# Ten norm factors take a way through scratch memory in place of a TensorE spread

## The chip, the cores and the metric

The kernel runs on one core of a Trainium2 chip. The time is device microseconds of one execution. The core's engines are TensorE (PE in the profile, its weight loads PEld), VectorE (DVE), ScalarE (ACT), GpSimd (POOL) and SyncE (SP); SP and ACT issue the DMAs, which sixteen DMA engines carry out. Each engine works through its own list of instructions in the order of the program; an instruction that has to wait holds up those behind it on its engine.

## The reference

One layer of an encoder over 2048 tokens of 1024 features: a gated short convolution, then a SwiGLU network of 2816 hidden features, each between two RMS norms and scaled, shifted and gated by vectors made from `c`.

```python
def rms_norm(x, g):
    y = x * lax.rsqrt(jnp.mean(x * x, axis=-1, keepdims=True) + RMS_EPS)
    return y * g

h = modulate(rms_norm(x, gains[0]), sh_m, sc_m)
h = short_conv_mixer(h, w_in, w_conv, w_out)       # 1024 -> 3072, conv of width 3, 1024 -> 1024
x = x + g_m * rms_norm(h, gains[1])
h = modulate(rms_norm(x, gains[2]), sh_f, sc_f)
h = swiglu(h, w_gate_up, w_down)                   # 1024 -> 5632, 2816 -> 1024
x = x + g_f * rms_norm(h, gains[3])
```

A norm's factor `rsqrt(mean + eps)` is one number per token, and it multiplies every feature of that token.

## The kernel before

Features lie on the 128 partitions and 512 tokens along the free axis. The 2048 tokens are two halves (`u` = 0, 1) of two token tiles each (`tok` = 0, 1) of 512. The eight phases in program order are in0, out0, in1, out1, gu0, down0, gu1, down1: the convolution's input and output projection for both halves, then the gate-up and down projection for both halves. Each product of 2x2 blocks is done by Strassen's seven products (P1 to P7), and each fp32 product as three matmuls on operands split into a high and a low part (`h` and `l` in tile names).

The work is a list of slots, one per product, about twelve matmuls of 128x512 each. The main loop walks the slots; in front of a slot it issues the supply of coming weights, the events scheduled for that slot, and whatever `later(n, f)` has put off by `n` slots; a generator that does `yield n` is resumed `n` slots later. Every engine keeps this order: nothing is reordered by a scheduler.

A factor is made by `norm_of_sums`: four tiny matmuls sum the squares over the partitions, so that token 128 t + p of the tile has its sum on partition p in column t, and a few tiny DVE and POOL instructions make `q`, 128x4, out of it. To multiply a 128x512 tile whose tokens lie along the free axis, the factors must stand as one row of 512 that is the same in all 128 partitions. That is what `spread_later` makes: `diagonal` writes four 128x128 blocks, the identity times a column of `q` (four DVE instructions); four slots later `spread` multiplies a 128x128 matrix of ones with the 128x512 result on PE into a PSUM bank, and ACT copies the bank into an SBUF tile `rb`, of which there are two buffers (`NRB`).

Fourteen factors are spread. Names: `r0` to `r3` for the first norm of each token tile; `n00` to `n11` (after out0 and out1, digits `u` and `tok`) for the second; `m00` to `m11` are the factors of the third, spread under the names `h00` to `h11` before gu0 and gu1; `o00` and `o01` (after down0) and `o10` (during down1) for the fourth; the very last one is made and spread by `last_half`. A tile name ends in `q` for the 128x4 factor, `d` for the diagonal, `b` for the PSUM bank and `r` for the row in all partitions.

Users of a row: after n, `after_out` loads the stored output tiles (`zz`) and input tiles (`xx`), multiplies `zz` by the row on DVE, adds, and stores the sum as `x1`. After h, `Features.scale` multiplies the tiles of the gu phase (`gu0a` to `gu0d`, `gu1a` to `gu1d`). After o, `after_down` finishes the output tiles (`zo`, `xo`).

DMAs of the stretch that the prediction speaks of: `in6P3k` and the like are kept weight operands of in1 loaded by SP, `kgu2P` the gu weights split ahead during in1 and stored by SP (ACT writes their buffers next), `y1A` and `y1S` stored operands for out1, `ada` rows for the conditioning vectors.

Of the kernel before, what the change touches and what calls it, by code (L numbers as in the profile page):

```python
# [10 lines left out]
F32 = mybir.dt.float32  # L11
# [4 lines left out]
P = 128  # L16
# [7 lines left out]
CH = 512  # L24
# [11 lines left out]
NBIG, NWP, NRAW, NTMP, NRB = 17, 7, 16, 10, 2  # L36
# [13 lines left out]
def hybrid_conv_layer(  # L50
# [31 lines left out]
    V, A, PE, G, SP = map(Engine, (nc.vector, nc.scalar, nc.tensor, nc.gpsimd, nc.sync))  # L82
# [4 lines left out]
    bigs, pairs, raws, sb = (ctx.enter_context(tc.tile_pool(name=n, bufs=1)) for n in ("bigs", "pairs", "raws", "sb"))  # L87
# [6 lines left out]
    def raw(name):  # L94
        return raws.tile([P, CH], F32, tag="raw", bufs=NRAW, name=name)
# [7 lines left out]
    def small(n, name):  # L103
        return sb.tile([P, n], F32, tag="small", bufs=16, name=name)

    def bank(name):
        return ps.tile([P, CH], F32, tag="mm", bufs=8, name=name)
# [5 lines left out]
    def later(slots, f):  # L113
        waiting.append((now[0] + slots, len(waiting), f))

    def run(gen):


        def step():
            n = next(gen, None)  # L120
            if n is not None:
                later(n, step)

        step()
# [38 lines left out]
    def col(t, k):  # L163
        return t[:, k : k + 1]
# [53 lines left out]
    def root(v, name):  # L218

        p, t = small(4, name + "p"), small(4, name + "t")  # L220
        G.tensor_tensor(p, v, mhalf, ALU.pow)
        yield 1
        q = sb.tile([P, 4], F32, tag="q", bufs=8, name=name + "q")
        V.tensor_tensor(t, p, p, ALU.mult)
        V.tensor_tensor(t, t, v, ALU.mult)
        V.scalar_tensor_tensor(q, t, -3.0, p, ALU.add, ALU.mult)
        return q
# [8 lines left out]
    def diagonal(q, name):  # L236
        dg = tmp(name + "d")
        for t in range(4):
            V.tensor_scalar(dg[:, t * P : (t + 1) * P], ident, q[:, t : t + 1], None, ALU.mult)
        return dg  # L240

    def spread(dg, name):
        ps_ = bank(name + "b")
        PE.matmul(ps_, one, dg[:, :CH], start=True, stop=True)
        rb = sb.tile([P, CH], F32, tag="rb", bufs=NRB, name=name + "r")
        A.copy(rb, ps_)
        return rb

    def spread_later(q, name, put, lag=4):
        dg = diagonal(q, name)  # L250
        yield lag
        put(spread(dg, name))

    def norm_of_sums(acc, name):

        st = bank(name + "s")
        for t in range(4):
            PE.matmul(st[:, t : t + 1], acc[:, t * P : (t + 1) * P], mean, start=True, stop=True)
        v = small(4, name + "v")
        V.tensor_scalar(v, st[:, :4], EPS, None, ALU.add)  # L260
        yield 1
        return (yield from root(v, name))
# [29 lines left out]
    def scratch(shape, name):  # L292
        return dram.tile(shape, F32, name=name)
# [586 lines left out]
    def schedule(slot, f):  # L880
        events.setdefault(max(slot, 0), []).append(f)
# [10 lines left out]
    for s in slots:  # L892
        ph = s.ph
        if ph.kind in ("out", "down"):
            w = Weight(ph.kind, s.grp, s.op, None, ks=s.ks)
        elif s.n < LEAD and ph.name != "in0" or ph.name == "in1" and s.g.i == 2:
            w = Weight(ph.kind, s.grp, s.op, None)
        else:
            b = of.setdefault((ph.name, s.n), Blocks(ph.kind, s.grp))
            w = Weight(ph.kind, s.grp, s.op, b, ph.name == "in0" and s.g.i in (1, 2),  # L900
                       whole_words=ph.name == "in0" and s.n < LEAD and s.op in UNSPLIT)
# [3 lines left out]
        if s.n >= LEAD and extra.get(ph.name) and len(position) > 7 * LEAD + 2 * (EARLY - LEAD):  # L905
            n = count[ph.name] = count.get(ph.name, 0) + 1
# [24 lines left out]
    rb1 = {}  # L931

    def put(d, key, rb):
        d[key] = rb

    def after_out(ph, tok):

        u = ph.u
        rb = {}
        yield 7  # L940
        q = yield from norm_of_sums(ph.acc[tok], f"n{u}{tok}")
        yield (24 if u == 0 else 34) + 8 * tok
        yield from spread_later(q, f"n{u}{tok}", partial(put, rb, 0))
        acc = {}
        tiles = {}

        def load(k):
            z, xt = raw(f"zz{u}{tok}{k}"), raw(f"xx{u}{tok}{k}")
            SP.dma_start(z, z_d[u][tok][:, k, :])
            SP.dma_start(xt, xt_d[u * 2 + tok, k // 4][:, (k % 4) * CH : (k % 4 + 1) * CH])  # L950
            tiles[k] = z, xt

        load(0)
        yield 1
        load(1)
        yield 2
        for k in range(KD):
            if k + 2 < KD:
                load(k + 2)
            z, xt = tiles.pop(k)  # L960
            V.scalar_tensor_tensor(z, z, col(mG[0], k), rb[0], ALU.mult, ALU.mult)
            V.tensor_tensor(xt, xt, z, ALU.add)
            later(2, partial(add_square, acc, 0, xt, f"nq{u}{tok}{k}"))
            later(3, partial(A.dma_start, x1_d[u][tok][:, k, :], xt))
            yield 2
        yield 7
        rb1[u, tok] = yield from norm_of_sums(acc[0], f"m{u}{tok}")

    def after_down(ph, tok):
        u = ph.u  # L970
        rb = {}
        if ph.last and tok:
            yield 1
            yield from last_half(ph)
            return
        yield 4 if ph.last else 7
        q = yield from norm_of_sums(ph.acc[tok], f"o{u}{tok}")
        if not ph.last:
            yield 22 + 10 * tok
        yield from spread_later(q, f"o{u}{tok}", partial(put, rb, 0), 2 if ph.last else 4)  # L980
        tiles = {}

        def load(k):
            xt = raw(f"xo{u}{tok}{k}")
            SP.dma_start(xt, x1_d[u][tok][:, k, :])
            if ph.last:
                z = ph.z(tok, k)
            else:
                z = raw(f"zo{u}{tok}{k}")
                SP.dma_start(z, z2_d[u][tok][:, k, :])  # L990
            tiles[k] = z, xt

        load(0)
        yield 1
        load(1)
        yield 2
        for k in range(KD):
            if k + 2 < KD:
                load(k + 2)
            z, xt = tiles.pop(k)  # L1000
            V.scalar_tensor_tensor(z, z, col(mG[1], k), rb[0], ALU.mult, ALU.mult)
            V.tensor_tensor(xt, xt, z, ALU.add)
            later(1, partial(A.dma_start, out_tile(u, tok, k), xt))
            yield 1.5 if ph.last else 2

    def out_tile(u, tok, k):
        return out[u * 2 + tok, k // 4][:, (k % 4) * CH : (k % 4 + 1) * CH]
# [44 lines left out]
    for ph in phases:  # L1052
        if ph.kind not in ("out", "down"):
            continue
        ph.zt = {}

        def z(tok, n, ph=ph):
            if (tok, n // 4) not in ph.zt:
                ph.zt[tok, n // 4] = big(f"{ph.name}z{tok}{n // 4}")
            return ph.zt[tok, n // 4][:, n % 4, :]  # L1060

        def tile_ready(tok, n, zt, ph=ph):
            if not ph.last:
                d = (z_d if ph.kind == "out" else z2_d)[ph.u][tok]
                later(1, partial(SP.dma_start, d[:, n, :], zt))

        def half_ready(tok, ph=ph):
            run((after_out if ph.kind == "out" else after_down)(ph, tok))

        ph.z, ph.tile_ready, ph.half_ready = z, tile_ready, half_ready  # L1070


    def from_xt(u):
        return lambda t, tok, kk: SP.dma_start(t, xt_d[u * 2 + tok, kk].rearrange("p (a b) -> p a b", a=4))
# [278 lines left out]
    for ph in phases[1:]:  # L1353
        f = first[ph.name]
        if ph.kind in ("out", "down"):
            loaded(ph, own[ph.name], f)
            continue
        turn = {}
        for i, s in enumerate(slots):
            if s.ph is ph and s.n == 0 and s.op not in turn:  # L1360
                turn[s.op] = i

        def at(op, off, fn, turn=turn):
            schedule(turn[op] + off, fn)

        if ph.kind == "in":
            rb_in = {}
            for tok in range(2):
                g = ph.u * 2 + tok
                schedule(f - 69 + 26 * tok, lambda g=g, tok=tok: run(norm_of_rows(g, f"r{g}", partial(put, rb_in, tok))))  # L1370
            normalized(Features(ph, from_xt(ph.u), rb_in, 0), at, 0)
        else:
            rb = {}
            src = lambda t, tok, kk, u=ph.u: SP.dma_start(t, x1_d[u][tok][:, kk * 4 : kk * 4 + 4, :])
            for tok, op in ((0, "P1"), (1, "P7")):
                go = lambda u=ph.u, tok=tok, rb=rb: run(spread_later(rb1[u, tok], f"h{u}{tok}", partial(put, rb, tok)))
                at(op, -14 - 2 * ph.u, go)
            normalized(Features(ph, src, rb, 1), at, 2 * ph.u)

    schedule(24, lambda: run(sums_later("out", range(4), 2)))  # L1380
# [98 lines left out]
```

## Time and profile before

| | |
|---|---|
| time, median of 3 runs | 1972.45 us (1971.13 to 1973.41) |
| span of the profiled execution | 1972.0 us; the profile gives no time of that execution outside its span |
| PE busy | 1940.5 us (98%) |
| DVE busy | 1466.1 us (74%) |
| ACT busy | 871.4 us (44%) |
| POOL busy | 340.7 us (17%) |
| DMA | 459.51 MB, 233 GB/s over the span |

All instructions carry line L78, which is the helper that records them, so they are told apart by tile names, with buffer numbers left out (`in1P` stands for all the PSUM banks of in1, `kgu2P` for all stored operands of weight group gu2). In a timeline or a chain the first number is the start in microseconds from the start of the span and the second the duration of the piece; `x4` counts merged instructions. A matmul's modelled end overlaps the next one, so the pace of PE is read from starts.

### The profile page before, as it was taken

Reading aid. Unit: us, or ns where it says so; the run is one execution under the profiler, and the core shown is the slowest. Engines: PE = TensorE matmul, PEld = TensorE weight load, DVE = VectorE, ACT = ScalarE, POOL = GpSimd, SP = SyncE. Lnnn points to the kernel's source line nnn. Section 1 sums busy time; section 2 is a strip of 40 time slices with the busy share of each in tenths; the row PEclk is TensorE's granted clock in tenths of the full one; section 3 lists DMA queues with packets and bytes.
Section 4 is the critical chain, followed back from the end, with each engine's and each line's share of the span. In section 5 each row is a group of like instructions: output and inputs, shape, how many; then the busy total and the mean of one; then the engine's idle time right before and its main releaser. Section 6 shows DMA issues by size and latency. Waiting matters only on the chain.

```text
span 1972.0 us, 24969 instructions
## 1 busy us (share of the span) xinstructions
PE 1940.5 (98%) x8460; PEld 1573.3 (80%) x8460; DVE 1466.1 (74%) x2159; ACT 871.4 (44%) x1430; POOL 340.7 (17%) x224
## 2 busy tenths in 40 slices
PE   7899999999999999999999999999999999999998
PEld 4578887777888888888888888888888888888886
DVE  4898888988998876898776755586776655665466
ACT  4543447534345653444333454463333333444452
POOL 0012202201221311243341310120100100111010
PEclk9999999999999999999999999999999999999999
DMA  9369859869996763677665887578564342386634
GB/s 389 126 224 374 312 187 350 320 226 367 327 320 221 272 245 126 231 238 244 210 221 190 295 291 269 188 272 277 187 197 141 122 145 97 115 313 228 199 134 132
DMA packets 204752, 459.51 MB, mean 233 GB/s; under 512 B 22864, under 2 KB 38352, under 8 KB 198224
## 3 DMA queue, kind: packets, MB, share of 16 engines
q1 hardware_dynamic: 180000, 403.52, 59.3%
q10 hardware_dynamic: 24624, 54.40, 7.2%
q8 instruction: 66, 1.08, 0.2%
q14 instruction: 62, 0.51, 0.1%
HBM read 326.75 MB, written 131.07 MB: 232 GB/s over the span
## 4 chain that ended last, share of the span: by engine, by line
PE 84%; DVE 6%; DMA 5%; issue 2%; ACT 2%; SPq 0%; POOL 0%; ACTq 0%; POOLq 0%; DVEq 0%
PE gu0P L78 21%; PE gu1P L78 21%; PE in0P L78 11%; PE down0P L78 11%; PE down1P L78 9%; PE in1P L78 5%; PE out1P L78 4%; PE out0P L78 1%; DMA kgu2P<-gu2P 1%; DVE ada L78 1%; DVE in1c L78 1%; DVE in1y L78 0%; DMA y1S<-in1b1s 0%; DMA in0a<-xt_d 0%; DMA c<-c_row_d 0%
## 5 line engine op out<-in xcount | busy, mean ns | idle before, releaser
L78 DVE TENSOR_TENSOR gu1a<-gu1P,gu1a 128x512 f32<-128x512 f32 x63 | 43.5, 691 | 108.6 <-PE gu1P L78 108.6
L78 DVE TENSOR_TENSOR gu0a<-gu0P,gu0a 128x512 f32<-128x512 f32 x63 | 43.3, 688 | 70.5 <-PE gu0P L78 68.5
L78 POOL TENSOR_TENSOR gu1a<-gu1a 128x512 f32<-128x512 f32 x11 | 19.0, 1728 | 363.4 <-DVE gu1g11s L78 42.5
L78 ACT COPY gu1a<-gu1P 128x512 f32<-128x512 f32 x42 | 24.7, 589 | 98.5 <-PE gu1P L78 87.3
L78 POOL TENSOR_TENSOR nq<-nq,nq 128x512 f32<-128x512 f32 x28 | 42.5, 1517 | 129.9 <-ACT nq L78 125.1
L78 ACT COPY gu0a<-gu0P 128x512 f32<-128x512 f32 x42 | 24.5, 588 | 83.7 <-PE gu0P L78 82.5
L78 DVE CUSTOM_DVE_ANT_0 ada<-ada,c 128x512 f32<-128x512 f32 x80 | 56.8, 720 | 0.0
L78 ACT COPY gu1g<-gu1P 128x512 f32<-128x512 f32 x24 | 14.1, 589 | 92.8 <-PE gu1P L78 92.8
L78 POOL TENSOR_TENSOR down0q<-down0q,down0q 128x512 f32<-128x512 f32 x14 | 23.9, 1705 | 144.1 <-ACT down0q L78 144.0
L78 ACT COPY gu0g<-gu0P 128x512 f32<-128x512 f32 x24 | 14.1, 589 | 76.9 <-PE gu0P L78 75.4
L78 POOL TENSOR_TENSOR gu0a<-gu0a 128x512 f32<-128x512 f32 x11 | 18.3, 1660 | 171.1 <-ACT gu0a L78 47.4
L78 POOL TENSOR_TENSOR down1q<-down1q,down1q 128x512 f32<-128x512 f32 x10 | 16.1, 1610 | 148.7 <-ACT down1q L78 148.6
L78 DVE TENSOR_TENSOR gu1g<-gu1P,gu1g 128x512 f32<-128x512 f32 x24 | 16.6, 692 | 27.4 <-ACT gu1g L78 26.0
L78 DVE TENSOR_TENSOR down2P<-down2P,down2P 128x512 fp32r<-128x512 f32 x14 | 11.9, 853 | 28.6 <-ACT down2P L78 28.6
L78 ACT ACTIVATE gu1a<-gu1a 128x512 f32<-128x512 f32 x42 | 26.6, 633 | 13.2 <-DVE xo L78 6.0
L78 ACT ACTIVATE gu0a<-gu0a 128x512 f32<-128x512 f32 x42 | 26.6, 634 | 11.1 <-DVE gu0a L78 9.3
L78 POOL TENSOR_TENSOR out1q<-out1q,out1q 128x512 f32<-128x512 f32 x14 | 22.3, 1592 | 52.0 <-ACT out1q L78 51.9
L78 POOL TENSOR_TENSOR out0q<-out0q,out0q 128x512 f32<-128x512 f32 x14 | 23.1, 1647 | 44.1 <-ACT out0q L78 44.0
L78 DVE TENSOR_TENSOR xx<-xx,zz 128x512 f32<-128x512 f32 x32 | 28.1, 878 | 1.1
L78 ACT ACTIVATE nq<-xx 128x512 f32<-128x512 f32 x32 | 20.2, 632 | 17.1 <-DVE xx L78 17.0
L78 DVE TENSOR_TENSOR gu0g<-gu0P,gu0g 128x512 f32<-128x512 f32 x24 | 16.5, 689 | 14.7 <-ACT gu0g L78 13.3
L78 DVE TENSOR_TENSOR down10P<-down10P,down10P 128x384 fp32r<-128x384 f32 x14 | 8.6, 615 | 22.3 <-ACT down10P L78 22.3
(3225 smaller groups left out, 6733.5 us busy)
## 6 DMA issues: line engine op xcount, KB each, us to landing
ada<-ada_d SPq DMA_DIRECT2D x64, 256.0 KB, 5.7
act0A<-gu0a SPq DMA_DIRECT2D x33, 256.0 KB, 3.4
act1A<-gu1a SPq DMA_DIRECT2D x33, 256.0 KB, 2.5
ada<-ada_d SPq DMA_DIRECT2D x16, 512.0 KB, 9.4
zz<-z SPq DMA_DIRECT2D x32, 256.0 KB, 5.3
xx<-xt_d SPq DMA_DIRECT2D x32, 256.0 KB, 5.4
x<-xx ACTq DMA_DIRECT2D x32, 256.0 KB, 5.5
down0S<-act0S SPq DMA_DIRECT2D x8, 1024.0 KB, 7.0
```

What stands on the lines that cost most here:

```text
L78: return tc.keep_in_program_order(f(*args, **kwargs))
```

## The change

In place of ten of the fourteen spreads (n, h and o, but not r, o10 and the last), the factor `q` is stored to a DRAM scratch of 512 floats eight slots after it was made, by SP, with `(t p) -> p t`, so that each of the 512 numbers lands at its token's place; each is a run of 4 bytes on the DRAM side. Later SP loads the scratch row into `rb` in all 128 partitions (each reads the same 2 KB), eight slots before the row is handed to its users. The load stands four slots ahead of the place where the diagonal was made, which in turn stood four slots ahead of the spread, so users get the row in the same slot as before. The diagonals, the ten matmuls with ones, their PSUM banks and the ten ACT copies are gone.

```diff
@@ -250,6 +250,18 @@
+    def keep_row(q, name):
+
+        row = scratch([CH], name + "w")
+        later(8, lambda: SP.dma_start(row.rearrange("(t p) -> p t", p=P), q))
+        return row
+
+    def repeat_later(row, name, put):
+        rb = sb.tile([P, CH], F32, tag="rb", bufs=NRB, name=name + "r")
+        SP.dma_start(rb, row.rearrange("(a n) -> a n", a=1).to_broadcast((P, CH)))
+        yield 8
+        put(rb)
@@ -939,8 +951,9 @@  after_out
         q = yield from norm_of_sums(ph.acc[tok], f"n{u}{tok}")
-        yield (24 if u == 0 else 34) + 8 * tok
-        yield from spread_later(q, f"n{u}{tok}", partial(put, rb, 0))
+        row = keep_row(q, f"n{u}{tok}")
+        yield (20 if u == 0 else 30) + 8 * tok
+        yield from repeat_later(row, f"n{u}{tok}", partial(put, rb, 0))
@@ -964,7 +977,8 @@
-        rb1[u, tok] = yield from norm_of_sums(acc[0], f"m{u}{tok}")
+        q = yield from norm_of_sums(acc[0], f"m{u}{tok}")
+        rb1[u, tok] = keep_row(q, f"m{u}{tok}")
@@ -975,9 +989,12 @@  after_down
         q = yield from norm_of_sums(ph.acc[tok], f"o{u}{tok}")
-        if not ph.last:
-            yield 22 + 10 * tok
-        yield from spread_later(q, f"o{u}{tok}", partial(put, rb, 0), 2 if ph.last else 4)
+        if ph.last:
+            yield from spread_later(q, f"o{u}{tok}", partial(put, rb, 0), 2)
+        else:
+            row = keep_row(q, f"o{u}{tok}")
+            yield 18 + 10 * tok
+            yield from repeat_later(row, f"o{u}{tok}", partial(put, rb, 0))
@@ -1373,8 +1390,8 @@
-                go = lambda u=ph.u, tok=tok, rb=rb: run(spread_later(rb1[u, tok], f"h{u}{tok}", partial(put, rb, tok)))
-                at(op, -14 - 2 * ph.u, go)
+                go = lambda u=ph.u, tok=tok, rb=rb: run(repeat_later(rb1[u, tok], f"h{u}{tok}", partial(put, rb, tok)))
+                at(op, -18 - 2 * ph.u, go)
```

Two places show what this does to the engines' lists. On PE, in gu0, between the last matmuls of one slot (weights gu7P) and the first of the next (gu8P), before:

```order
L78 MATMUL gu0P_7_7070<-gu0S1h,gu7P_7095 128x512 x2
L78 MATMUL gu0P_7_7070<-gu0S1l,gu7P_7095 128x512
L78 MATMUL n11b<-n11d,one 128x512
L78 MATMUL gu0P_8_7258<-gu0A11h,gu8P_7118 128x512 x2
L78 MATMUL gu0P_8_7258<-gu0A11l,gu8P_7118 128x512
```

The same place after the change:

```order
L78 MATMUL gu0P_7_7049<-gu0S1h,gu7P_7074 128x512 x2
L78 MATMUL gu0P_7_7049<-gu0S1l,gu7P_7074 128x512
L78 MATMUL gu0P_8_7228<-gu0A11h,gu8P_7097 128x512 x2
L78 MATMUL gu0P_8_7228<-gu0A11l,gu8P_7097 128x512
```

The matmul with ones is gone and its neighbours follow each other; the other nine places on PE read alike, and nothing else on PE moves. On SP, late in in1, the list of DMAs before:

```order
L78 DMA kgu2P_4750<-gu2P_4716 128x1024
L78 DMA y1S_111<-in1b0s_4711 128x512
L78 DMA ada_0_2_4810<-ada_d 128x512
L78 DMA y1S_112<-in1y_3902 128x512
L78 DMA y1S_113<-in1b0s_4712 128x512
L78 DMA y1A_107<-in1y_4085 128x512
L78 DMA y1A_108<-in1y_4085 128x512
L78 DMA ada_0_3_4855<-ada_d 128x512
L78 DMA kgu2P_4830<-gu2P_4804 128x1024
```

After the change, with the store of the factor m00 as 512 single numbers:

```order
L78 DMA kgu2P_4741<-gu2P_4707 128x1024
L78 DMA y1S_111<-in1b0s_4702 128x512
L78 DMA ada_0_2_4801<-ada_d 128x512
L78 DMA y1S_112<-in1y_3899 128x512
L78 DMA m00w<-m00q 128x4x1
L78 DMA y1S_113<-in1b0s_4703 128x512
L78 DMA y1A_107<-in1y_4082 128x512
L78 DMA y1A_108<-in1y_4082 128x512
L78 DMA ada_0_3_4847<-ada_d 128x512
L78 DMA kgu2P_4821<-gu2P_4795 128x1024
```

One row is new, five DMAs ahead of a `kgu2P` store. Ten such stores (`w` in the name) and ten loads of a row stand in SP's list in all.

## The prediction

> **What bounds the kernel now.** I read the page's busy shares first, then busy time by stretch, then who made PE wait, then the chain of waits where PE did wait. The page, its busy line and the main DMA queue:
>
> ```profile
> span 1972.0 us, 24969 instructions
> PE 1940.5 (98%) x8460; PEld 1573.3 (80%) x8460; DVE 1466.1 (74%) x2159; ACT 871.4 (44%) x1430; POOL 340.7 (17%) x224
> q1 hardware_dynamic: 180000, 403.52, 59.3%
> ```
>
> The busy time by stretch (start:end, length, then PE, PEld, DVE, ACT, POOL, the granted clock, the DMA share and GB/s):
>
> ```profile
> 400.00:445.00 45.00, 42.95 (x188) 34.91 (x187) 38.36 (x72) 17.53 (x28) 0.51 (x1) 1.00 0.67 230
> 445.00:470.00 25.00, 23.80 (x104) 19.05 (x103) 19.93 (x34) 9.88 (x19) 2.42 (x2) 1.00 1.02 352
> 470.00:512.00 42.00, 42.00 (x185) 34.24 (x184) 40.88 (x61) 17.49 (x30) 9.96 (x7) 1.00 0.96 352
> 512.00:570.00 58.00, 57.78 (x263) 47.78 (x262) 57.34 (x86) 22.09 (x39) 16.10 (x11) 1.00 0.97 334
> 600.00:680.00 80.00, 80.00 (x354) 65.44 (x353) 68.12 (x103) 49.80 (x85) 19.50 (x12) 1.00 0.70 241
> 680.00:1100.00 420.00, 420.00 (x1863) 347.46 (x1862) 328.53 (x427) 169.58 (x291) 126.75 (x82) 1.00 0.65 215
> 1100.00:1320.00 220.00, 220.00 (x972) 181.65 (x971) 143.37 (x194) 112.72 (x163) 35.45 (x24) 1.00 0.74 266
> 1320.00:1735.00 415.00, 415.00 (x1832) 343.06 (x1831) 274.86 (x403) 151.95 (x259) 36.71 (x23) 1.00 0.49 166
> ```
>
> Two regimes are to be seen. From 600 us on PE never stops, at full clock, and DMA and DVE have room: whatever leaves PE's list there leaves the time. From 445 to 570 us, the second half of in1, the sixteen DMA engines are full (0.96 to 1.02), DVE is at 97 to 99% from 470 on, and PE only just keeps up. The waits of PE in 400 to 470 and 470 to 620:
>
> ```profile
> PE in1P L78 <- ACT in1c L78: 2.1, 2, 1.2
> PE in1P L78 <- DMA in6P3k<-kin6P: 1.2, 1, 1.2
> PE in1P L78 <- ACT in1C L78: 0.2, 1, 0.2
> ```
>
> In each row stand the total, the number of times and the longest. The second ends at 467.71 and the last at 569.00, as the chain has it:
>
> ```profile
> 442.97 0.79 DVE n00d L78 x4
> ...
> 459.99 7.58 DMA in6P3k<-kin6P
> ...
> 467.71 24.89 PE in1P L78 x108
> 492.60 0.86 PE n01b L78 x2
> ...
> 560.99 6.24 DMA kgu2P<-gu2P
> ...
> 569.00 6.19 PE in1P L78 x26
> ```
>
> **What is removed outside in1.** Eight of the ten spreads (h00 at 653.7 us to o01 at 1440.6) lie where PE never waits. One of them in PE's timeline:
>
> ```profile
> 831.37 0.39 PE L78 MATMUL gu0P<-gu0S1l,gu7P 128*128 128x512 f32 x1
> 831.60 0.62 PE L78 MATMUL gu0P<-gu0S1h,gu7P 128*128 128x512 f32 x2
> 832.05 0.40 PE L78 MATMUL gu0P<-gu0S1l,gu7P 128*128 128x512 f32 x1
> 832.29 1.02 PE L78 MATMUL n11b<-n11d,one 128*128 128x512 f32 x2
> 832.75 1.03 PE L78 MATMUL gu0P<-gu0A11h,gu8P 128*128 128x512 f32 x2
> 833.61 0.39 PE L78 MATMUL gu0P<-gu0A11l,gu8P 128*128 128x512 f32 x1
> ```
>
> Three ordinary matmuls take 832.05 - 831.37 = 0.68 us; with the spread (one matmul in the program, two passes in the trace) among them it is 833.61 - 832.05 = 1.56. A spread costs PE 0.88 us, and eight of them **7.0 us**. The gain is kept if nothing else starts to hold PE, and the stretches say so: DVE at 66 to 85% and DMA at 49 to 74% are the cover. The four diagonal instructions and the ACT copy that also leave bring nothing there, since PE waits for neither.
>
> **What is removed in in1.** n00 and n01 lie on a path that DMA and DVE share. The diagonal of n00 stands on the chain with 0.79 us ahead of the wait that ends at 467.71. Without it that wait can end 0.79 earlier; PE itself comes 0.88 earlier and then waits 0.1 longer than now. The spread of n01 is on the chain with 0.86. If nothing were added, PE would go on at 569.00 - 1.65. The diagonal of n01, about 0.8 more on a DVE that is nearly full, I cost at nothing: behind it the chain runs over DMAs.
>
> **What is added in in1.** Five DMAs, three in front of or beside the full stretch and two in it. SP's timeline, where n01's row is loaded (right behind in7P2k) and where m00 is stored (between the two y1S):
>
> ```profile
> 477.40 0.32 SPq L78 DMA_DIRECT2D in7P2k<-kin7P  x1
> ...
> 557.26 1.19 SPq L78 DMA_DIRECT2D y1S<-in1y  x1
> 558.54 0.41 SPq L78 DMA_DIRECT2D y1S<-in1b0s  x1
> ```
>
> The load of n01's row moves 128 x 2 KB = 262 KB; at the 352 GB/s of its stretch that is **0.74 us** of all sixteen engines, and since they are full it comes on top. Bounds: 0 (the stores behind it have slack) to 0.74; I take 0.74. n00's row is loaded near 420 us, where the DMA share is 0.67, and its store and n01's go out near 390 and 411 us: cost nothing, covered by that room, and at most what m00's costs if the cover is gone.
>
> m00's store is 512 packets of 4 bytes, 32 per DMA engine. The trace has no such DMA. From above I bound a packet by the mean of the main queue, 0.593 x 16 x 1972.0 / 180000 = 0.104 us for packets of 2.2 KB on average: 32 x 0.104 = 3.3 us of every engine. From below it is nothing. A packet has a part that goes with its bytes and a part that doesn't, and no row separates them; I take the middle, **1.7 us**. Page "DMA: Bandwidth & Descriptors" of the Trainium skill, section "Measured", has a floor of 0.68 us for 64 packets; by an estimate from it 32 packets cost 0.34 us and the forecast would be 1.4 us lower. No run here shows it yet.
>
> Who is behind the store: ACT has to wait for the kgu2P store issued at 560.99 before it may overwrite the buffer, and PE's wait at 569.00 hangs on ACT:
>
> ```profile
> 567.32 0.62 ACT L78 CAST gu2P<-gu2b 128x512 fp32r<-128x512 f32 x1 [5.39 <-DMA kgu2P<-gu2P]
> 567.85 0.62 ACT L78 CAST in9P<-in9b 128x512 fp32r<-128x512 f32 x1
> 568.38 0.57 ACT L78 COPY in1C<-in1P 128x512 f32<-128x512 f32 x1
> ```
>
> ACT sits 5.39 us idle for that DMA, so any delay of it is PE's delay, undamped. In1 together: -0.79 - 0.86 + 0.74 + 1.7 = **+0.8 us**, between -1.65 (nothing added counts) and +2.4 (3.3 us for the store).
>
> **What is added elsewhere costs nothing.** A store must not wait long for its factor and a row must land before its use, into a free buffer:
>
> ```profile
> L78 DVE SCALAR_TENSOR_TENSOR m00q<-m00t,m00p x1: 164/164/164, 532.4 to 532.4; 128x4 f32<-128x4 f32 x1
> L78 DVE SCALAR_TENSOR_TENSOR zz<-zz,mG,n01r x8: 739/746/1784, 509.2 to 550.4; 128x512 f32<-128x512 f32 x8
> L78 DVE SCALAR_TENSOR_TENSOR gu1b<-gu1b,mA,h10r x4: 746/748/749, 1302.2 to 1304.7; 128x512 f32<-128x512 f32 x4
> L78 ACT COPY o00r<-o00b x1: 588/588/588, 1348.3 to 1348.3; 128x512 f32<-128x512 f32 x1
> c<-c_row_d SPq DMA_DIRECT2D x8, 256.0 KB, 5.4
> ```
>
> m00's factor is ready 26 us before SP comes to its store. A load like the new one (c, one row into 128 partitions) lands in 5.4 us; n01's is issued at 478 for a use at 509. The tightest buffer is o00's: eight slots of twelve matmuls (8 x 12 x 0.227 = 22 us) ahead of 1348 is 1326, and the row that held it, h10's, was last read at 1305. If such a load did stall, SP would hold all later weights, but they run some slots ahead.
>
> **Sum.** -7.0 + 0.8 = -6.2 us against the span of 1972.0; the median of the runs stands 0.45 above that span, and I take this offset as unchanged: 1972.45 - 6.2 = **1966.2 us**.
>
> **The rivals.** (1) *All is gained.* Small packets cost little and in1's path shortens as PE does: 10 x 0.88 = 8.8 us, 1963.6. For it speaks that n00d and n01b both stand on the chain and leave it; against it the DMA share of 0.96 to 1.02 with five DMAs more. (2) *In1 gives it back.* A 4-byte packet costs as much as a 2 KB one, and of the stores of n00 and n01 one reaches PE too: 3.3 + 3.3 + 0.74 - 1.65 = +5.7, so 1972.45 - 7.0 + 5.7 = 1971.1, no change. PE's waits on ACT before 445 speak for a thin margin there, the DMA share of 0.67 against it. (3) *Slower by the small stores.* If a 4-byte write costs more than a packet of 2 KB, m00's store alone holds every engine while ACT waits: at 0.5 us a packet 16 us, 1972.45 - 7.0 - 1.65 + 0.74 + 16 = 1980.5. The gain is gone from 7.9 us per store (0.25 us a packet), and it is slower beyond doubt from 11.8 (0.37). No row has a packet so dear. The section "Specifications" of that page of the Trainium skill says that under 512 bytes a DMA engine reads, modifies and writes, which is a reason for a dearer packet; no trace here shows it. (4) That the spreads don't leave can be ruled out: ten rows are gone from PE's list, and none came.
>
> **How the numbers follow.** Chances: forecast 0.47, (1) 0.25, (2) 0.18, (3) 0.10. About 0.2%, 3.9 us, is what a measurement of this kernel can tell from no change. Faster beyond it: the forecast, (1) and a third or so of (2)'s spread towards less, 0.78; the same 0.14, from the rest of (2) and the mild end of (3); slower 0.08. The likeliest case alone goes from 1963.8 (in1 at -1.65) to 1967.8 (in1 at +2.4); the range takes in (1) and most of (2): 1962.8 to 1970.5.
>
> **What would show it.** The steps are right if in the changed profile PE stays without a wait from 600 to 1900 us, the ordinary matmul pace runs through the eight places, and the start of down0's first matmul moves by the four spreads of gu0 and out1 (3.5 us) plus what in1 gives. m00w's time from issue to landing and the wait of PE near 569 tell in1's term: the forecast has that wait 1.5 to 2.5 us long, (1) under 0.5, (2) above 4. It is wrong if PE gains waits on a `zz`, `gu0a` or `zo` tile that waits for a row, on weights behind an SP that stands at one of the new DMAs, or if the stores of n00 and n01 lengthen PE's waits before 445 us.

## The result: slower, and the profile after

| | before | after |
|---|---|---|
| median of five runs each | 1972.45 us (1970.61 to 1973.41) | 1982.39 us (1981.29 to 1984.17) |
| ratio after / before, 95% interval | | 1.0053 (1.0042 to 1.0063) |
| span of the profiled execution | 1972.0 us | 1980.6 us (its time 1982.89) |
| PE / DVE / ACT busy | 1940.5 / 1466.1 / 871.4 us | 1933.9 / 1456.9 / 864.6 us |

The kernel became 9.9 us slower where 6.2 us less was foretold. The page of the changed kernel begins:

```profile
span 1980.6 us, 24897 instructions
PE 1933.9 (98%) x8440; PEld 1570.2 (79%) x8440; DVE 1456.9 (74%) x2119; ACT 864.6 (44%) x1420; POOL 341.8 (17%) x224
q1 hardware_dynamic: 186720, 406.16, 60.8%
```

PE has its twenty passes less (8460 to 8440), 6.6 us less work, and yet ends 8.6 us later: it waits more. SP's queue has 6720 packets more, which is ten times 512 for a store, 128 for a load, and 32 beside the data. Who made PE wait, after (total, times, longest):

```profile
PE in1P L78 <- ACT in1C L78: 7.2, 1, 7.2
...
PE gu0P L78 <- ACT gu0g L78: 4.4, 1, 4.4
...
PE in1P L78 <- ACT in1c L78: 2.1, 2, 1.3
...
PE in1P L78 <- DMA in6P3k<-kin6P: 2.0, 1, 2.0
PE gu1P L78 <- ACT gu1a L78: 1.1, 1, 1.1
```

The first was 0.2 us before, the second wasn't there. Where in the program the time went is read best from the first starts of six groups of matmuls, one from each phase (each row: shortest, median and longest in ns, then first and last start in us). Before:

```profile
L78 PE MATMUL out0P<-out0S,out1P x16: 389/389/393, 308.5 to 346.0; 128*128 128x512 f32 x16
L78 PE MATMUL out1P<-out1S,out0P x16: 389/389/393, 626.9 to 662.5; 128*128 128x512 f32 x16
L78 PE MATMUL gu0P<-gu0A11h,gu0P1k x8: 389/389/389, 683.6 to 685.8; 128*128 128x512 f32 x8
L78 PE MATMUL down0P<-down0S,down0P x16: 389/389/389, 1167.3 to 1259.1; 128*128 128x512 f32 x16
L78 PE MATMUL gu1P<-gu1A11h,gu0P1k x8: 389/389/389, 1319.1 to 1321.4; 128*128 128x512 f32 x8
L78 PE MATMUL down1P<-down1S,down0P x16: 389/389/389, 1801.0 to 1892.8; 128*128 128x512 f32 x16
```

After:

```profile
L78 PE MATMUL out0P<-out0S,out1P x16: 389/389/393, 307.7 to 345.3; 128*128 128x512 f32 x16
L78 PE MATMUL out1P<-out1S,out0P x16: 389/389/397, 634.5 to 669.2; 128*128 128x512 f32 x16
L78 PE MATMUL gu0P<-gu0A11h,gu0P1k x8: 389/389/389, 689.4 to 691.7; 128*128 128x512 f32 x8
L78 PE MATMUL down0P<-down0S,down0P x16: 389/389/389, 1178.5 to 1270.3; 128*128 128x512 f32 x16
L78 PE MATMUL gu1P<-gu1A11h,gu0P1k x8: 389/389/389, 1328.5 to 1330.8; 128*128 128x512 f32 x8
L78 PE MATMUL down1P<-down1S,down0P x16: 389/389/389, 1810.1 to 1901.9; 128*128 128x512 f32 x16
```

The start of out0 lies ahead of the change and differs by 1 to 3 us from one execution to the next, so the lengths between the rows are compared. The last four columns are the experiments below, read from the same rows of their traces:

| stretch, us | spreads in it before | before | after | e1 | e2 | e12 | e10 |
|---|---|---|---|---|---|---|---|
| out0 to out1 (holds in1) | n00, n01 | 318.4 | 326.8 | 318.4 | 324.6 | 318.7 | 317.4 |
| out1 to gu0 | h00, h01 | 56.7 | 54.9 | 54.8 | 56.6 | 55.7 | 54.9 |
| gu0 to down0 | n10, n11 | 483.7 | 489.1 | 482.8 | 487.9 | 482.2 | 484.2 |
| down0 to gu1 | h10, h11 | 151.8 | 150.0 | 150.1 | 151.8 | 150.9 | 150.1 |
| gu1 to down1 | o00, o01 | 481.9 | 481.6 | 480.1 | 481.9 | 480.2 | 480.1 |
| sum | | 1492.5 | 1502.4 | 1486.2 | 1502.8 | 1487.7 | 1486.7 |

The sum rises by 9.9 us, as the median does. Where nothing else happened (out1 to gu0, down0 to gu1) two spreads are worth 1.8 us, 0.9 each. Two stretches lost: in1 8.4 us and gu0 5.4. A third, gu1, gives back 0.3 us where e1 gives 1.8: PE waits 1.1 us there on `gu1a`. That wait goes back to o01's store, too: a load of `zo` that SP issues 1.4 us behind it lands after 12.9 us, DVE waits for it, then ACT for DVE, and PE for ACT's `gu1a`.

**In1.** The chain of waits of the changed kernel near the loss, with start and duration:

```profile
560.44 12.44 DMA kgu2P<-gu2P
...
574.66 25.54 PE in1P L78 x103
```

ACT's timeline behind it (idle time and what ended it in brackets):

```profile
572.98 0.62 ACT L78 CAST gu2P<-gu2b 128x512 fp32r<-128x512 f32 x1 [11.51 <-DMA kgu2P<-gu2P]
573.51 0.61 ACT L78 CAST in9P<-in9b 128x512 fp32r<-128x512 f32 x1
574.03 0.58 ACT L78 COPY in1C<-in1P 128x512 f32<-128x512 f32 x1
```

The `kgu2P` store that took 6.24 us before takes 12.44, ACT is idle for 11.51 in place of 5.39 ahead of the same cast, and PE stands 7.2 us for the copy two instructions further on. What stands ahead of `kgu2P` in SP's list is m00's store, and the views of the two tiles `m00w` and `m10w` say how long it was under way. In these rows the longer time is the store's and the shorter one the later load's; m00w first, then m10w:

```profile
DMA to landing us min/median/max: 7.0/9.3/11.6
DMA to landing us min/median/max: 7.5/9.3/11.2
```

Over all ten stores the mean is 11.2 us (9.2 to 12.8); the forecast's 1.7 us of all engines, or 3.3 at most, was meant to cover that.

**Gu0.** The chain there:

```profile
893.85 11.20 DMA m10w<-m10q
905.05 0.02 issue
905.07 0.33 ACTq L78
905.40 0.04 issue
905.44 0.59 ACT gu0g L78
906.03 0.04 issue
906.08 5.99 PE gu0P L78 x18
```

ACT has a DMA of its own to issue, a store of `x`, and comes to it only when m10's store has landed: 5.53 us idle. Nothing in that store of `x` needs m10's factor. The order with its semaphores shows the link, a semaphore that both wait for:

```
L78 DMA m10w<-m10q 128x4x1 [waits DMAHW4_49]
L78 DMA x_135<-xx_7577 128x512 [waits DMAHW4_49]
```

In the trace, too, the `x` store waits for the semaphore that m10's store raises. In this program eight semaphores go round over all DMAs of SP and ACT together. The `x` store is the eighth DMA after m10's and takes over its semaphore, so it must wait for its landing, with ACT's copy `gu0g` behind it and PE behind that.

**What happened on the DMA engines and to the clock.** Busy time by stretch of the changed kernel (columns as in the prediction), around the two places and in the long stretches:

```profile
564.00:568.00 4.00, 3.44 (x18) 2.59 (x17) 3.96 (x7) 0.00 (x0) 0.88 (x1) 1.00 0.52 29
574.00:578.00 4.00, 3.34 (x8) 2.67 (x9) 4.00 (x11) 2.26 (x5) 0.51 (x1) 0.50 1.06 366
578.00:582.00 4.00, 4.00 (x18) 3.25 (x17) 3.11 (x8) 1.73 (x3) 0.51 (x1) 0.91 1.05 406
600.00:680.00 80.00, 80.00 (x353) 65.94 (x352) 67.05 (x97) 50.22 (x84) 16.81 (x10) 1.00 0.67 231
680.00:1100.00 420.00, 415.08 (x1839) 343.45 (x1838) 322.31 (x418) 165.95 (x288) 119.48 (x78) 1.00 0.67 215
900.00:904.00 4.00, 1.68 (x8) 1.06 (x6) 2.55 (x3) 0.00 (x0) 1.31 (x1) 1.00 0.27 34
904.00:908.00 4.00, 1.92 (x5) 1.58 (x6) 1.89 (x3) 1.12 (x2) 0.35 (x1) 0.80 0.55 146
908.00:912.00 4.00, 4.00 (x15) 3.13 (x14) 2.83 (x5) 3.20 (x6) 1.95 (x2) 0.77 0.97 336
1100.00:1320.00 220.00, 220.00 (x976) 182.32 (x975) 142.85 (x181) 109.15 (x156) 41.70 (x27) 1.00 0.75 265
```

Two of the same stretches before:

```profile
564.00:568.00 4.00, 4.00 (x23) 3.40 (x23) 3.93 (x8) 0.68 (x2) 0.00 (x0) 1.00 0.95 339
574.00:578.00 4.00, 4.00 (x20) 3.30 (x19) 4.00 (x11) 2.61 (x5) 1.02 (x1) 1.00 1.04 406
```

In the four microseconds from 564 on, while the store is under way, the core moves 29 GB/s where it moved 339, and from 900 on it moves 34; over the whole landing of m00's store (557.6 to 569.2) it is 131 in place of 349. The engines hold packets, but few bytes pass. And each of the two long stalls of PE is followed by a second loss. After the 7.2 us the granted clock is 0.50; the eleven matmuls from 574.66 on take until 579.17, 4.5 us where the full pace of 0.227 us makes 2.5: **2.0 us**. The eleven from 906.08 to 910.29 take 4.2 in place of 2.5: **1.7 us**. For these two stalls the rows bear out the Trainium skill, page "TensorE: Matmul & The Clock Gate", section "Why this matters for your kernels": an idle gap of PE of more than about 3 us brings the clock back to half. The runs below don't all fit that figure: in e4 waits of 3.7, 2.0 and 1.9 us are each followed by a granted clock of 0.57 to 0.65 in the next 4 us, while after waits of 3.1 us in e2 (gu0) and in e7 (in1) it stays at 1.00. So the length of the wait alone doesn't decide here.

In1 then adds up: 7.0 more wait on `in1C`, 2.0 of clock, 0.8 more on `in6P3k`, less 1.8 for two spreads, 8.0 of the 8.4 measured. Gu0: 4.4 + 1.7 - 1.8 = 4.3 of 5.4. Of the 1.1 that is missing 0.5 is a wait of PE on `gu0a` at 723.67, which the kernel before doesn't have and which e1 has as well (at 712.97), where the two spreads of that stretch bring 0.9 in place of 1.8. For that wait and for the rest I have no cause.

### The profile page after: what moved, and what is told of

It is laid out like the page before. It is cut to its first block, busy times and chain, and to the rows that moved or that the text cites. A ratio compares the mean times of both kernels' runs of the same rounds, so it can differ in the third digit from the quotient of the medians.

```text
span 1980.6 us, 24897 instructions
## 1 busy us (share of the span) xinstructions
PE 1933.9 (98%) x8440; PEld 1570.2 (79%) x8440; DVE 1456.9 (74%) x2119; ACT 864.6 (44%) x1420; POOL 341.8 (17%) x224
## 3 DMA queue, kind: packets, MB, share of 16 engines
q1 hardware_dynamic: 186720, 406.16, 60.8%
## 4 chain that ended last, share of the span: by engine, by line
PE 78%; DVE 11%; DMA 5%; issue 3%; ACT 3%; SPq 0%; POOL 0%; ACTq 0%; POOLq 0%; DVEq 0%
PE gu1P L78 21%; PE gu0P L78 15%; PE down0P L78 11%; PE in0P L78 9%; PE down1P L78 9%; PE in1P L78 7%; PE out1P L78 2%; PE out0P L78 2%; DVE gu0a L78 1%; PE pms L78 1%; DMA kgu2P<-gu2P 1%; DMA m10w<-m10q 1%; DMA ada<-ada_d 1%; DVE in1y L78 0%; DVE in1c L78 0%
## 5 line engine op out<-in xcount | busy, mean ns | idle before, releaser
L78 DVE TENSOR_TENSOR gu0g<-gu0P,gu0g 128x512 f32<-128x512 f32 x24 | 16.5, 690 | 18.2 <-ACT gu0g L78 16.8
L78 ACT ACTIVATE nq<-xx 128x512 f32<-128x512 f32 x32 | 20.2, 631 | 16.8 <-DVE xx L78 16.8
```

Source lines behind the costliest of these rows:

```text
L78: return tc.keep_in_program_order(f(*args, **kwargs))
```

## The experiments

The theory after the result: the loss is all the stores', their long landing comes from how the 512 numbers lie in the scratch memory, and it reaches PE only where something that PE needs is queued behind. The rivals were a price per packet (512 of them, wherever they go), the ten loads, and a price for the removal itself, such as DVE or ACT coming earlier into somebody's way. Each run is compared with the kernel before on the same chip.

### e1: the same number of bytes in 128 packets

Each partition's four factors are stored as one run of 16 bytes. The factors then reach other tokens than their own, so this kernel computes something else; its instructions and their times are those of the change.

```diff
-        later(8, lambda: SP.dma_start(row.rearrange("(t p) -> p t", p=P), q))
+        later(8, lambda: SP.dma_start(row.rearrange("(p t) -> p t", t=4), q))
```

> The changed kernel with one thing different: the factor is stored as 128 runs of 16 bytes (partition by partition) in place of 512 runs of 4 bytes. The numbers lie in another order in the row, so the factors reach the wrong tokens; work and sizes are otherwise the same. Theory A (the number of packets of the store is the price): the store lands in 4 to 6 us in place of 9 to 13, PE's waits of 7.2 us in in1 and 4.4 us in gu0 go away, time 1963 to 1967. Theory B (a store of 2 KB is dear whatever its packets): time stays at 1980 to 1984, landing 9 us and more. Theory C (the loads into all partitions are the price): time stays at 1980 to 1984, but the stores land fast.

Measured 1964.76 us, ratio 0.9965 (0.9952 to 0.9977): 6.9 us faster than before, where the forecast of the change was 6.2. m00's store lands in 4.8 us, the ten in 5.2 on average. The `kgu2P` store in the chain of e1 is back, and PE's long waits on ACT's `in1C` and `gu0g` are gone from the list of its waits:

```profile
558.20 5.91 DMA kgu2P<-gu2P
```

One changed access pattern takes away the whole loss, so it isn't the removal, the loads or the place of the stores as such. In the table above e1 and before differ by 0.0 in in1 and by the spreads elsewhere (less 0.9 in gu0).

### e2 and e3: the stores alone, the loads alone

e2 adds the ten stores to the kernel before, which keeps its spreads (the diff shows the place of n's). e3 keeps the spreads too and adds the ten loads, of the first 512 numbers of `c`, into the buffer that the spread later overwrites.

```diff
@@ e2, against before
         q = yield from norm_of_sums(ph.acc[tok], f"n{u}{tok}")
+        keep_row(q, f"n{u}{tok}")
         yield (24 if u == 0 else 34) + 8 * tok
...
@@ e3, against before
+    def load_and_spread(q, name, put):
+        rb = sb.tile([P, CH], F32, tag="rb", bufs=NRB, name=name + "r")
+        SP.dma_start(rb, c_row[:, :CH].to_broadcast((P, CH)))
+        yield 4
+        dg = diagonal(q, name)
+        yield 4
+        put(over(dg, rb, name))
```

> The kernel before with the ten 4-byte stores added at the places that the change has them; nobody reads them, and the spreads on TensorE stay. Theory A (the stores are the price): the changed kernel lost 9.9 us although 8.8 us of spreads are gone, so the stores cost about 18 us: 1988 to 1993, with PE waits near 570 us and 900 us. Theory C (the loads): 1972 to 1974. A third, that the stores only hurt in the places where a spread was taken away: 1975 to 1985.

> The kernel before with the ten loads of a 2 KB row into all partitions added where the change has them (half of c's row, into the row buffer, which ScalarE's copy of the spread then overwrites). Theory A (the stores): 1972 to 1974, at most the 0.74 us of the load in the full stretch. Theory C (the loads): 1981 to 1991.

e3: 1971.63 us, 1.0002 (0.9993 to 1.0011). The loads cost nothing that can be measured. e2: 1983.38 us, 1.0062 (1.0047 to 1.0077). The stores alone cost 11.7 us, in the same two places. PE's waits in e2:

```profile
PE in1P L78 <- ACT in1C L78: 4.5, 1, 4.5
PE gu0P L78 <- ACT gu0g L78: 3.1, 1, 3.1
```

The size missed: with the spreads' 8.8 us taken back, the change's loss would be 9.9 + 8.8 = 18.7. By the table, in1 costs 6.2 us here (324.6 against 318.4) and 8.4 between e1 and the change; gu0 4.2 and 6.3. The prices don't add, and the traces show in part where they differ. In e2 the stores of m00 and m10 land in 10.2 and 10.0 us, where the change has 11.6 and 11.2; PE's waits are 2.7 and 1.3 us shorter; in gu0 the clock stays full behind the wait, and gu1 loses nothing. Why the stores land sooner beside the spreads isn't shown.

### e5, e8, e11 and e7: how the numbers lie

All four keep the 512 packets of 4 bytes and put them further apart in a larger scratch. Their loads read the first 512 numbers of `c` in place of the stored factors, so the rows hold other numbers; that part of the computation is left out.

```diff
@@ e5: 512 bytes apart (e8: a=16, 64 bytes; e11: a=2, 8 bytes)
-        row = scratch([CH], name + "w")
-        later(8, lambda: SP.dma_start(row.rearrange("(t p) -> p t", p=P), q))
-        return row
+        row = scratch([128 * CH], name + "w")
+        later(8, lambda: SP.dma_start(row.rearrange("(t p a) -> p t a", p=P, a=128)[:, :, 0], q))
+        return c_row[0, :CH]
@@ e7: 8 bytes apart, the four numbers of a partition side by side
+        row = scratch([2 * CH], name + "w")
+        later(8, lambda: SP.dma_start(row.rearrange("(p t a) -> p t a", p=P, a=2)[:, :, 0], q))
+        return c_row[0, :CH]
```

> The changed kernel with the 512 numbers stored 512 bytes apart in a scratch of 256 KB, in place of side by side in 2 KB; the loads read half of c's row, so the factors are not used and the output is another. Theory A1 (a 4-byte packet has its price wherever it lands): the store lands in 9 to 13 us, time 1980 to 1984. Theory A2 (packets of several DMA engines that write into the same few hundred bytes wait for each other): the store lands in 4 to 6 us and the time is 1963 to 1967.

> The changed kernel with 512 numbers of 4 bytes, 64 bytes apart in 32 KB, in the order of the change (t, then p). The loads read half of c's row, the factors are not used. Theory A2 with a block of 64 bytes or less: lands in 4 to 6 us, 1963 to 1967. With a larger block (up to the 512 bytes that were shown to be enough): landing 7 to 12 us, 1968 to 1984.

> The changed kernel with 512 numbers of 4 bytes, 8 bytes apart, in partition order in 4 KB: the four numbers of a partition are neighbours, the partitions follow each other. The loads read half of c's row, the factors are not used. Theory A2a (what is dear is that partitions which different DMA engines serve write into the same few bytes): neighbours are now mostly of one partition, the store lands in 4 to 7 us, 1963 to 1967. Theory A2b (many 4-byte writes into a small area are dear, whoever makes them): landing 9 to 13 us, 1978 to 1984.

> The changed kernel with 512 numbers of 4 bytes, 8 bytes apart in 4 KB, in the order of the change (t, then p), so that eight neighbours in 64 bytes are of eight partitions; with the same distance in partition order they were of two. The loads read half of c's row, the factors are not used. Theory A3 (what counts is how many writes fall into 64 bytes: 16 landed in 11.2 us on average, 8 in 7.7, 1 in 5.1): 7 to 8.5 us, time 1969 to 1973. Theory A2a (writes of different partitions collide more): 9 to 11 us, 1975 to 1982.

| kernel | packets of a store | numbers in one block of 64 bytes | mean landing of ten stores, us | m00w, us | median, us | ratio (95%) |
|---|---|---|---|---|---|---|
| after | 512 | 16 | 11.2 | 11.6 | 1982.39 | 1.0053 (1.0042 to 1.0063) |
| e7 | 512 | 8, from two partitions | 7.7 | 7.9 | 1971.24 | 0.9999 (0.9990 to 1.0008) |
| e11 | 512 | 8, from eight partitions | 7.2 | 6.7 | 1966.74 | 0.9981 (0.9971 to 0.9991) |
| e8 | 512 | 1 | 5.1 | 4.0 | 1964.61 | 0.9964 (0.9951 to 0.9976) |
| e5 | 512 | 1 (512 bytes apart) | 4.7 | 4.0 | 1964.69 | 0.9968 (0.9957 to 0.9979) |
| e1 | 128 | 16, written four at a time | 5.2 | 4.8 | 1964.76 | 0.9965 (0.9952 to 0.9977) |

The view of the tile m00w in e8, where the loads don't read it, so that the row is the store's alone:

```profile
DMA to landing us min/median/max: 4.0/4.0/4.0
```

The same row of e11:

```profile
DMA to landing us min/median/max: 6.7/6.7/6.7
```

e5 and e8 have the change's 512 packets of 4 bytes, to the packet, and land as fast as e1 with 128: a price per packet, or for writes of 4 bytes as such, falls. What counts is how close together the single writes lie. Counted by blocks of 64 bytes, a store lands (7.4 - 5.1)/7 = 0.33 us later for each further write in a block at eight (mean of e7 and e11), (11.2 - 5.1)/15 = 0.41 at sixteen. e7 and e11 differ in whether neighbours come from the same partition or from eight; the writes of eight partitions land no later (7.2 against 7.7), so that isn't it. That 64 bytes is the size that counts, and not some smaller one above 8, no run tells. e1 speaks for a smaller one: with four writes of 16 bytes in 64 it would land at 5.1 + 3 x 0.33 = 6.1 us, and it lands at 5.2.

The trace's records of single DMA packets show who pays. A packet of 4 bytes takes 9 ns in the median in every one of these kernels, the change too; at that, the 32 that an engine has of a store make 0.3 us. What lengthens is packets of 2 KB beside and behind the stores: between 350 and 1400 us, 238 of them take over 1 us in the change (the longest 6.3), 150 in e7, 105 in e11, and 54 to 62 in e8, e5 and e1, as in the kernel before (58).

The times don't follow the landings evenly. From 4.0 to 6.7 us of m00w the median moves by 2.1 us, from 6.7 to 7.9 by 4.5. PE's waits on `in1C` and `gu0g` are 0.8 and 0.5 us in e11, 3.1 and 2.0 in e7. The landing of m10's store less the wait on `gu0g` is 6.8 us in e11, e7 and the change alike (7.3 - 0.5, 8.8 - 2.0, 11.2 - 4.4); for m00's and `in1C` it is 5.9, 4.8 and 4.4. So there is a slack of 4 to 7 us behind these stores, and only what is longer reaches PE. The landings are those of one execution each, e11's of its fastest, so the step from e11 to e7 is rough.

### e12: which of the ten stores cost

m00 and m10 are spread on PE as before; the other eight factors take the change's way, with its slow stores.

```diff
-        rb1[u, tok] = keep_row(q, f"m{u}{tok}")
+        rb1[u, tok] = keep_row(q, f"m{u}{tok}") if tok else q
...
+                way, ahead = (repeat_later, 18) if tok else (spread_later, 14)
```

> The changed kernel with m00 and m10 spread on TensorE as before; the other eight factors take the way through scratch, with stores of 4 bytes. Theory E (of the ten slow stores only the two that the milestones show cost time): eight spreads less, 8 x 0.88 = 7.0, and about 1 us of small waits: 1965 to 1967. Theory E' (the other slow stores cost too, hidden behind the two): 1969 to 1976.

Measured 1966.97 us, 0.9977 (0.9968 to 0.9986). It is 2.2 us above e1, and the two spreads that it keeps are 1.8 of them; in the table its stretches are e1's within 0.6 us but for those two spreads. Yet its stores are as slow as the change's: n00's takes 12.8 us, n11's 11.2. Here the eight other slow stores cost nothing that can be seen; the two that are gone had somebody behind them. In the change one of the eight, o01's, cost 1.1 us; it landed in 12.2 us there and in 9.5 in e12.

### e9: m10's store one slot later

```diff
-        later(8, lambda: SP.dma_start(row.rearrange("(t p) -> p t", p=P), q))
+        later(9 if name == "m10" else 8, lambda: SP.dma_start(row.rearrange("(t p) -> p t", p=P), q))
```

> The changed kernel with one DMA issued one slot later: the store of m10. Eight DMA semaphores go round over the DMAs of both queues, and the eighth DMA after a given one waits for it. In the changed kernel that is ScalarE's store of x1 behind m10's store, and ScalarE stands 5.5 us; one slot later it is a store that SP issues. Theory D (ScalarE's wait on the shared semaphore is what costs the 6.4 us in gu0): the wait of TensorE on the gu0g copy near 905 us goes away, 1975 to 1978. Theory D' (the slow store holds the DMA engines and anything behind it is late): the wait stays, perhaps on another tile, 1980 to 1984.

Measured 1978.33 us, 1.0037 (1.0024 to 1.0051), between the times of the two theories; the runs (1976.65 to 1981.67) touch those of the change. The trace is of the slowest of the four. In it the wait on `gu0g` is gone, as a round of semaphores would have it, and another stands in its place. ACT's timeline of e9, and its row among PE's waits:

```profile
906.65 0.62 ACT L78 CAST gu10P<-gu10b 128x512 fp32r<-128x512 f32 x1 [8.11 <-DMA gu12b<-w_gu_d]
```

```profile
PE gu0P L78 <- ACT gu0a L78: 5.0, 2, 4.6
```

The stretch from gu0 to down0 is 489.8 us long, 0.7 more than in the change. ACT now waits for a load of `gu12b` that SP issues right behind m10's store and that lands no sooner than the store: ACT's own store `kdown0P`, ahead of the cast, takes over that load's semaphore. So in this execution the theory that the one link from m10's store was the cause doesn't hold; what gu0 looked like in the three shorter ones isn't recorded. Everything behind such a store is late, on its own queue and, through the shared round of semaphores, on ACT's; which of these PE meets first depends on the place. It agrees with the Trainium skill, page "DMA: Bandwidth & Descriptors", section "Queues, rings and completion order": the write that raises a DMA's semaphore lands on an engine only after every earlier write of that engine. The traces add that what stands shortly ahead is late as well: in the change a `y1S` that SP issued 0.75 us ahead of m00's store landed after 10.5 us (the same one in e1 after 4.2), and a store of ACT's, `out_d`, issued 2.3 us ahead of o01's, after 14.3.

### e4, e6 and e10: three ways to store runs and keep the tokens in order

e4 turns `q` on PE into 4x128, which ACT copies and SP stores as four runs of 512 bytes. e6 takes the sums' weights with a step of four columns, so that partition p holds four neighbouring tokens, and stores runs of 16 bytes. e10 reaches the same order by letting ACT write the squares turned.

```diff
@@ e4
+            PE.matmul(b[:4, :P], q, ident, start=True, stop=True)
+            A.copy(t[:4, :P], b[:4, :P])
+            later(4, lambda: SP.dma_start(row.rearrange("(t p) -> t p", p=P), t[:4, :P]))
@@ e6, in norm_of_sums (the store as in e1)
+                a = acc[:, :CH].rearrange("p (n t) -> p n t", t=4)[:, :, t]
@@ e10, in add_square (the store as in e1)
+                to = to[:, :CH].rearrange("p (t n) -> p n t", t=4)
+                A.activation(to, z.rearrange("p (n t) -> p n t", t=4), AF.Square)
```

> The changed kernel, whole: TensorE turns the 128x4 factor into 4x128 (one small matmul with the identity), ScalarE copies it out, and SP stores four runs of 512 bytes. Theory A: stores land in 2 to 6 us and TensorE gives back 0.2 to 0.4 us of 0.88 per factor: 1966 to 1969. Theory C' (any scratch round trip with a load into all partitions costs): 1975 and above.

> The changed kernel, whole and with the reference's output: the four small matmuls of a norm take every fourth token (t, t+4, ...) in place of 128 in a row, so that partition p holds tokens 4p to 4p+3 and the factor is stored in token order as 128 runs of 16 bytes. Theory A (packets of 4 bytes that lie side by side are the price): as with the 16-byte runs before, 1963 to 1967, stores land in 4 to 7 us. If the weight load of a tile with a step of 16 bytes is dear, the sums' matmuls lengthen (0.8 us before, twelve of them): up to 1970.

> The changed kernel, whole and with the reference's output: ScalarE writes the squares of a tile in turned order (token 4p+t into column 128t+p), so that the sums' matmuls load their weights from 128 neighbours as before, partition p holds tokens 4p to 4p+3, and the factor goes out in token order as 128 runs of 16 bytes. If ScalarE's write with a step of 512 bytes takes no longer than its plain one (0.63 us), the time is that of the 16-byte runs, 1963 to 1966. If each square lengthens by half or more (0.3 us, 80 of them, off TensorE's path except in in1): 1966 to 1972.

e4: 1974.82 us, 1.0016 (1.0007 to 1.0025), 6 to 9 us more than expected. Its trace has no landing for its stores (the 3.8 to 5.9 us under their names are the loads'); PE's long waits on `in1C` and `gu0g` are gone. But the turning is a new matmul that comes when the factor may not be ready, and PE waits in order:

```profile
PE n00b L78 <- DVE n00q L78: 3.7, 1, 3.7
...
PE n10b L78 <- DVE n10q L78: 2.0, 1, 2.0
```

e6: 1970.03 us, 0.9993 (0.9984 to 1.0001), no change. Its stores are fast too; the gain goes to the strided weights. The load of one of m00's sums in e6, and the same row before:

```profile
L78 PEld LDWEIGHTS m00s<-mean,nq x8: 308/329/329, 517.5 to 519.1; 128*128 128x128 f32 x8
```

```profile
L78 PEld LDWEIGHTS m00s<-mean,nq x8: 187/192/193, 520.3 to 521.2; 128*128 128x128 f32 x8
```

The eight loads in the trace start over 1.6 us in place of 0.9, so each norm costs PE 0.7 us more, nearly a spread.

e10: 1965.10 us, 0.9969 (0.9958 to 0.9981). It is faster than the kernel before and than the change. Its price falls on ACT. The squares for the m factors in e10, and before:

```profile
L78 ACT ACTIVATE nq<-xx 128x512 f32<-128x512 f32 x32 | 37.0, 1157 | 14.6 <-DVE xx L78 14.6
```

```profile
L78 ACT ACTIVATE nq<-xx 128x512 f32<-128x512 f32 x32 | 20.2, 632 | 17.1 <-DVE xx L78 17.0
```

A square takes 1157 ns in place of 632, 16.8 us over these 32, on an engine that is 44% busy; PE's wait on `gu0a` grows to 1.5 us and that is all that shows.

## Why the prediction was wrong, step by step

**"From above I bound a packet by the mean of the main queue"** is the step that failed. It gave m00's store 3.3 us at most, and the forecast 1.7; the store took 11.6 us to land, and in1's stretch is 8.4 us longer than with fast stores (e1), where the term with both its ends had room for 3.3. The mean was of 2-KB packets that go to 2 KB of their own, and the store's price comes from single writes that lie side by side, a thing no row of the trace before held. For the store's own packets the term was large enough: they take 9 ns in the median, some 0.3 us of an engine in all. What was wrong is the mechanism. The forecast had the store occupy the engines for the sum of its packets; in the trace it holds up the transfers beside and behind it, whose 2-KB packets lengthen. Between e5 and the change SP's queue goes from 59.2% of 1962.1 us to 60.8% of 1980.6, 42.6 us of sixteen engines, 0.13 us for each of the 320 single writes that an engine has in the ten stores; that is over the bound of 0.104. The landing is longer by 6.5 us, 0.20 a write. What waits for a store pays its landing, and the forecast priced engine time.

**"What is added elsewhere costs nothing"** failed for two stores of the nine other than m00's. I asked whether the factor was ready, the row landed and the buffer free, and all that was so: PE has no wait on a row, and e3 finds no time for the loads. I didn't ask who is queued behind the other stores as I did for m00's. m10's is the dear one, with PE's 4.4 us for `gu0g`; o01's costs 1.1 for `gu1a`. Both lie behind 600 us, where "PE stays without a wait" was the sign to look for. The bound from above for a lost cover ("at most what m00's costs") was given for n00's and n01's stores alone.

**"Any delay of it is PE's delay, undamped"** was right in mechanism and short in price. The place, the store of `kgu2P`, the cast and the copy behind it are the ones that the prediction quoted, and 6.2 us more on the store made 7.0 more on PE. The clock at half behind it, 2.0 us here and 1.7 in gu0, was not in the sum at all.

**"A spread costs PE 0.88 us"** was right: 1.8 us for two in the two undisturbed stretches, and e1, e5, e8 and e10 come to 6.4 to 7.0 us less than before, against the 6.2 forecast. The four of gu0 and out1 brought 2.8 and not 3.5 (e1: 56.7 - 54.8 + 483.7 - 482.8). **In1 without a slow store**, -0.9 in the sum without its 1.7, is 0.0 in e1 and -1.0 in e10.

**The rivals.** (3) is what happened: 1980.5 foretold, 1982.39 measured, with a chance of 0.10. Its step was half right: the store holds what is behind it, and 11.6 us is over the 7.9 from which it was to eat the gain. Wrong were its reason, a 4-byte packet that is dearer wherever it goes, and its place, in1 alone. The Trainium skill's rule of that sentence (page "DMA: Bandwidth & Descriptors", section "Specifications": below 512 bytes a DMA engine reads, modifies and writes) is not what decides here: e8's packets are as small and land in 5.1 us. The estimate of 0.34 us from that page's section "Measured" fits the store's own packets (32 at 9 ns are 0.29 us), but it is far below even e8's store as a landing. (1), 8.8 us less, didn't come true even with the numbers laid out differently; those kernels lie at the forecast. (2), a loss in in1 alone of 5.7 us, had too little in1 and no gu0. (4) stays excluded.

**Still open:** what inside the DMA engines or the memory makes writes into one block queue up (only landings and the length of packets were measured); the exact size of the block, 64 bytes or less; the wait on `gu0a` and the rest of what the two spreads of gu0's stretch don't bring; why the stores land sooner in e2; and when a short wait of PE halves the clock.

## What to carry to other kernels

Before costing a small store, look where its numbers land: 512 single numbers side by side took 11.2 us, the same number of packets 64 bytes apart 5.1, and runs of 16 bytes 5.2; so choose the order of tokens such that a partition's numbers make one run, where an engine with room can pay for it. Then read what stands behind each such DMA, on its own queue and, where DMAs share a round of semaphores, on the other one too: of ten slow stores here two cost nearly all, one cost 1.1 us and seven nothing that can be seen. And price a long stall of PE with its clock: after 7.2 and 4.4 us it cost about 2 us on top.

## What the hardware did that I had not expected

- Single 4-byte writes that lie close together delay a store's landing by 0.33 to 0.41 us for each further one in 64 bytes (e7, e8, e11, after), while 512 of them in blocks of their own are as quick as 128 runs of 16 bytes (5.1 and 5.2 us).
- Such a store, 2 KB in all, brought the core's traffic from 349 GB/s to 131 while it was under way, and to 29 in four microseconds of it. Its own packets took 9 ns in the median; 2-KB packets beside and behind it took up to 6.2 us.
- A DMA issued 0.75 us ahead of such a store landed late as well, after 10.5 us (4.2 in e1).
- Weight loads from fp32 with a step of 16 bytes took 329 ns in place of 192 (e6), and ACT's squares written with a step of 512 bytes between neighbours 1157 in place of 632 (e10).
